# Cross-attention keys of the sample sequences loaded in 128-byte pieces and transposed by the vector engine, with three smaller edits

## The chip, the cores and the metric

The kernel runs on one core of a Trainium2 chip. A core has the engines PE (TensorE: matrix products), DVE (VectorE), ACT (ScalarE) and POOL (GpSimd), a sync engine SP, and 16 DMA engines. Each engine works through its own list of instructions in order. The metric is the device time of one execution in microseconds (us).

## The reference, cut to what matters

One step of a hybrid decoder layer, for a prompt of 256 tokens and for eight sample sequences of 4 tokens each (288 tokens in all, d_model 2048). An SSD branch and a GLA branch, both with a state per sample sequence, are merged by gates; then cross-attention into 256 memory tokens per sequence, then a ConvFFN (2 x 5632 columns, a convolution over 3 rows, the first two being carried rows from a state).

```python
def _cross_attend(hn, mem_k, mem_v, w_cq, w_co):
    q = (hn @ w_cq).reshape(Bsz, L, CROSS_HEADS, CROSS_HEAD_DIM)     # 4 heads of 512
    s = jnp.einsum('blhd,bmhd->bhlm', q, mem_k) * (CROSS_HEAD_DIM ** -0.5)
    pr = jax.nn.softmax(s, axis=-1)
    o = jnp.einsum('bhlm,bmhd->blhd', pr, mem_v)
    return o.reshape(Bsz, L, D_MODEL) @ w_co
# prompt: mem_k, mem_v computed from mem_prompt; samples: cache_mem_k, cache_mem_v (8, 256, 4, 512), read from memory
```

All data are float32. The keys are stored token by token, with the 512 numbers of a head side by side. The scores need the sum over these 512, and PE sums over partitions, so each key tile of 128 tokens x 128 numbers has to be transposed.

## The kernel before, in words

All large products are projections: `proj` loads a weight tile over SP's queue (512 KB, 24 matmuls of 128 x 288), splits it into a high and a low part (ACT L103, DVE L105) and multiplies each with the activations (L147, L148, L151). The stages follow each other: the input projection with the SSD scan, the GLA scan, the gates and the mix, the cross-attention, and the FFN. The work of the scans is woven into projections, which run in the background: a generator yields after a piece of work, and `weave` (L172) takes as many background units, of 12 matmuls each, as the numbers N_MAIN and N_BG (L38, L39) ask for. A scheduler then orders the instructions of each engine; the final order is fixed when the kernel is built.

Cross-attention is `attend(hd)` (L1379), once for each of the four heads, with the projections of the queries (w_cq) and of the output (w_co) around it:

- `loads` is the list of a head's tiles of memory: the keys of eight sequences (kc), keys and values of the prompt (kp, vp) and the values of sequences 4 to 7 (vc). Each is one DMA on POOL of 512 KB (L1376), 128 partitions x 2 token tiles x 512 numbers, and lies in one of five buffers `x4` that all of these share. `rows()` keeps four ahead. The values of sequences 0 to 3 (vq, L1411) have a buffer of their own and are loaded on POOL too.
- each key tile is transposed by PE (`transpose_half`, L1346, with L1352): eight transposes of 128 x 128 into two PSUM tiles, which one DVE copy and one ACT copy bring to kT (L1409).
- `scores(q)` (L1397) multiplies four sequences at a time: for each of four d-tiles and each sequence j one matmul (L1401), which writes the 32 rows of PSUM partition group j.
- the prompt's keys are transposed by PE and multiplied (L1430 to L1432), softmax of the samples runs, the weights are transposed (L1454), and L1463 multiplies them with vc and vq; that frees the buffers of vc for the next head.

The other lines that the change touches: the GLA scan of a head reads the states of eight sequences in two halves, four buffers `sin` (L1036), which L1138 multiplies, L1147 and L1148 update, an SP DMA writes back, and a POOL DMA fills again for the second half. `nudge(n)` (L119) puts two transposes of the identity, with n rows, into PE's order; `nudge(72)` stands at L1276 behind the first half of the gates and `nudge(P)` (L1548) before the FFN. The carried rows of the FFN are loaded at L1523 into `fin` (eight DMAs on POOL, 88 KB each, in pieces of 128 bytes), turned by DVE at L1535 into `fst`, all at once, and used by `ffn_conv` in `ffn_up`. FFN columns are worked in six blocks, of up to 8 tiles (BLK). In the SSD scan the states are already loaded as `sqr` in pieces of 128 bytes (L727) and turned by a DVE transpose (L878): it transposes each 32 x 32 square of a tile in its place, so that the DMA has to bring the squares to their places.

Of the kernel before, what the change touches and what calls it, by code (L numbers as in the profile page):

```python
# [8 lines left out]
F32 = mybir.dt.float32  # L9
# [7 lines left out]
P = 128  # L17
# [3 lines left out]
NB = 8  # L21
NL = 4
NS = NB * NL
# [18 lines left out]
@with_exitstack  # L42
def hybrid_step(ctx: ExitStack, tc: tile.TileContext, I: dict, O: list):
# [222 lines left out]
    with pool("p0") as p0:  # L266
# [95 lines left out]
        r = 0  # L362
# [217 lines left out]
    def b2(name):  # L580
        return pa.tile([P, 512], F32, tag="b2", bufs=10, name=name)
# [447 lines left out]
    def gla_scan(h, eb, qe, ke, kd, kde, vT, sr):  # L1029
# [104 lines left out]
        for q in range(2):  # L1134
            for k in (1, 0):
                for j in (3, 2, 1, 0):
                    b = 4 * q + j
                    MM(osa[NS * j:NS * j + NS, :], qdm[:, k, b, :], sins[b][:, k, :], start=False,  # L1138
                       stop=(q == 1 and k == 0))
            yield  # L1140
            for b in range(4 * q, 4 * q + 4):
                sin = sins[b]
                kb = pa.tile([P, 256], F32R, tag="kb", bufs=2, name="kb")
                V.tensor_scalar(kb, kst, bmask[:, b:b + 1], None, ALU.mult)
                for k in range(2):
                    a = mm_tile()
                    MM(a, kb[:, k * P:(k + 1) * P], vst, start=True, stop=True)  # L1147
                    V.scalar_tensor_tensor(sin[:, k, :], sin[:, k, :], eb[:, k, SEQ + 4 * b + 3:SEQ + 4 * b + 4], a,  # L1148
                                           ALU.mult, ALU.add)
                    yield 1.25  # L1150
                nc.sync.dma_start(out=o_sgla[b, h].rearrange("(k p) v -> p k v", p=P), in_=sin)
# [96 lines left out]
    def bigr2(name):  # L1248
        return pb.tile([P, KT, T], F32R, tag="bigr2", bufs=2, name=name)
# [124 lines left out]
    def mem_rows(src, name):  # L1374
        t = x4(name)
        G.dma_start(out=t, in_=src.rearrange("(m p) d -> p m d", p=P))  # L1376
        return t

    def attend(hd):  # L1379


        xq = xqm[hd % 2]
        loads = [(I["cache_mem_k"][b, :, hd, :], "kc") for b in range(NB)]
        loads += [(o_pmk[0, :, hd, :], "kp"), (o_pmv[0, :, hd, :], "vp")]
        loads += [(I["cache_mem_v"][b, :, hd, :], "vc") for b in range(4, NB)]
        got = []
        vq = big.tile([P, 4, 2, 512], F32, tag="bigf", bufs=1, name="vq")

        def rows():
            while loads and len(got) < 4:  # L1390
                got.append(mem_rows(*loads.pop(0)))
            return got.pop(0)

        ssc = la_tile()
# [2 lines left out]
        def scores(q):  # L1397
            for d in range(4):
                for j in (3, 2, 1, 0):
                    b = 4 * q + j  # L1400
                    MM(ssc[NS * j:NS * j + NS, 0:256], xq[:, d, b, :], kT[b][:, d, :], start=(q == 0 and d == 0),  # L1401
                       stop=(q == 1 and d == 3))

        for b in range(NB):
            kc = rows()
            kT.append(k4("kT"))
            for d2 in range(2):
                a = transpose_half(kc, d2)
                (S.copy if d2 else V.tensor_copy)(kT[b][:, 2 * d2:2 * d2 + 2, :], a)  # L1409
# [95 lines left out]
    fst = pf.tile([P, FT, 2, 16], F32, name="fst")  # L1505
    hf = halves(bigr, "hf")
    h = bigf("h")
    for j2 in range(KT // 2):
# [10 lines left out]
    fin = pf.tile([P, FT, 32], F32, name="fin")  # L1519
    crows = I["state_ffn_conv"].rearrange("b k c -> (b k) c").rearrange("r (i t g p) -> i g r t p", i=2, g=4, p=32)  # L1520
    for i in range(2):
        for g in range(4):
            G.dma_start(out=fin[32 * g + 16 * i:32 * g + 16 * i + 16], in_=crows[i, g])  # L1523

    def ffn_cols():
        for i0 in (0, 4):
            a = mm_tile()
            for i in range(i0, min(5, i0 + 4)):
                TR(a[:, (i - i0) * P:(i - i0 + 1) * P], frow[:, i, :], ident)
            if i0 == 0:  # L1530
                V.tensor_copy(fcol, a.rearrange("p (a t) -> p a t", t=P)[:, :, 0:88])
            else:
                V.tensor_copy(gfin, a[:, 0:KT])
        for t0 in range(0, FT, 11):
            V.transpose(fst[:, t0:t0 + 11].rearrange("p t i r -> p (t i r)"),  # L1535
                        fin[:, t0:t0 + 11].rearrange("p t c -> p (t c)"))

    run(*wo[:5])
    late.append(ffn_cols)
# [42 lines left out]
    blocks = [(0, FT % BLK)] + [(b0, BLK) for b0 in range(FT % BLK, FT, BLK)]  # L1582

    def ffn_up(b0, n):
        pr = bigr2("pr")
        c = cin[(b0 + BLK - 1) // BLK % 2]
        for q0 in range(b0, b0 + n, 4):
            for j2 in range(2):
                av = [pf.tile([P, T], F32, tag="av", bufs=4, name="av") for _ in range(2)]

                def consa(j, a, j2=j2, av=av):
                    t = 2 * j2 + j
                    ffn_conv(q0 + t, a, av[j], fst[:, q0 + t, 0, :], c[:, 0, q0 - b0 + t, 0:18])

                def consg(j, a, j2=j2, av=av):
                    t = 2 * j2 + j
                    gv = pf.tile([P, T], F32, tag="gv", bufs=3, name="gv")
                    ffn_conv(FT + q0 + t, a, gv, fst[:, q0 + t, 1, :], c[:, 1, q0 - b0 + t, 0:18])
# [126 lines left out]
```

## Time and profile before

| | |
|---|---|
| median of 3 runs | 2558.31 us (2558.08 to 2559.57) |
| the profiled execution | 2558.59 us, its span 2556.9 us |
| mean granted clock of PE | 0.997 |
| DMA | 521.95 MB, mean 204 GB/s |
| POOL's DMA queue (q0) | 96.37 MB, 12.2% of the 16 engines' span |
| SP's DMA queue (q1) | 422.34 MB, 53.8% |

One execution is recorded by the hardware profiler. A row of the groups names line, engine, operation, output and input, the count, then busy us and mean ns of one, then the idle time of the engine ahead of it and what ended most of it. Matrix products of float32 count twice in the profile where they are made in two passes (L1352, L1401, L1463). The page's view of 40 slices (64 us each) shows what the DMA engines do along the span; slices 23 to 26 hold the cross-attention:

```profile
DMA  7766587776868585777666778755555555555553
GB/s 263 219 223 200 169 243 213 225 210 201 231 190 295 173 258 160 244 234 231 187 208 210 251 261 303 213 178 171 168 173 168 172 167 174 169 170 172 169 172 128
```

### The profile page before, as it was taken

The page shows a single profiled execution, that of the slowest core. Times are in us where ns is not written, and L with a number is a line of the kernel's source. Part 1 is how long each engine was busy: PE and PEld are TensorE (multiplying, and loading weights), DVE is VectorE, ACT ScalarE, POOL GpSimd, SP SyncE. Part 2 cuts the span into 40 slices and gives each one's busy share as a digit, 9 for nine tenths or more (in the row PEclk, how much of TensorE's full clock was granted, in tenths as well). Part 3 has the DMA queues.
Part 4 walks back from the last instruction along what each step waited for, and adds up shares of the span by engine and source line. Part 5 has one row for each costly group of instructions (what it writes and reads, how often), then busy time and mean ns, then how long its engine had stood idle before and what let it go on. Part 6 is the DMA issues. An engine that isn't in the chain of part 4 may idle for free.

```text
span 2556.9 us, 50431 instructions
## 1 busy us (share of the span) xinstructions
PE 2536.4 (99%) x18968; PEld 2438.1 (95%) x18968; DVE 1731.3 (68%) x3670; ACT 1351.5 (53%) x2712; POOL 380.1 (15%) x701
## 2 busy tenths in 40 slices
PE   9999999999999999999999999999999999999998
PEld 8889999999999999989999989899999999999998
DVE  6656777796867566766566555567777677675765
ACT  7656547646454554544455544456545455454545
POOL 3002234242200000010000122201010101010010
PEclk9999999999999999999999999999999999999999
DMA  7766587776868585777666778755555555555553
GB/s 263 219 223 200 169 243 213 225 210 201 231 190 295 173 258 160 244 234 231 187 208 210 251 261 303 213 178 171 168 173 168 172 167 174 169 170 172 169 172 128
DMA packets 441125, 521.95 MB, mean 204 GB/s; under 512 B 26492, under 2 KB 389212, under 8 KB 440816
## 3 DMA queue, kind: packets, MB, share of 16 engines
q1 hardware_dynamic: 407728, 422.34, 53.8%
q0 software_dynamic: 33120, 96.37, 12.2%
q8 instruction: 149, 2.44, 0.4%
q14 instruction: 96, 0.79, 0.1%
q10 hardware_dynamic: 32, 0.01, 0.0%
HBM read 473.13 MB, written 45.48 MB: 203 GB/s over the span
## 4 chain that ended last, share of the span: by engine, by line
PE 96%; DMA 2%; DVE 1%; ACT 0%; POOL 0%; issue 0%; DVEq 0%; POOLq 0%; ACTq 0%
PE acc L148 27%; PE acc L147 26%; PE acc L151 26%; PE acc L315 2%; PE acc L316 2%; PE acc L319 2%; PE mm L1352 1%; PE la L1138 1%; PE la L1401 1%; PE la L1463 1%; PE mm L1111 1%; PE mm L1147 1%; DMA raw<-in_w_co_dram 0%; DMA sin<-in_state_gla_dram 0%; DMA out_dram<-sin 0%
## 5 line engine op out<-in xcount | busy, mean ns | idle before, releaser
L105 DVE TENSOR_TENSOR wlo<-raw,whi 128x512 fp32r<-128x512 f32 x1464 | 997.4, 687 | 662.0 <-ACT whi L103 634.7
L103 ACT CAST whi<-raw 128x512 fp32r<-128x512 f32 x1464 | 896.8, 618 | 1017.9 <-PE acc L148 792.7
L147 PE MATMUL acc<-xn,whi 128*128 128x288 f32 (+1 forms) x1936 | 550.0, 299 | 0.0
L148 PE MATMUL acc<-xn,whi 128*128 128x288 f32 (+1 forms) x1936 | 542.0, 296 | 0.0
L151 PE MATMUL acc<-xn,wlo 128*128 128x288 f32 (+1 forms) x1936 | 414.1, 295 | 0.0
L148 PE MATMUL acc<-hf,whi 128*128 128x288 f32 x1408 | 393.1, 295 | 0.0
L147 PE MATMUL acc<-hf,whi 128*128 128x288 f32 x1408 | 389.0, 292 | 0.0
L147 PEld LDWEIGHTS acc<-xn,whi 128*128 128x128 f32 (+1 forms) x1936 | 364.4, 188 | 9.7 <-issue 7.2
L148 PEld LDWEIGHTS acc<-xn,whi 128*128 128x128 f32 (+1 forms) x1936 | 364.6, 188 | 6.6 <-issue 4.8
L151 PEld LDWEIGHTS acc<-xn,wlo 128*128 128x128 f32 (+1 forms) x1936 | 310.4, 188 | 1.4 <-issue 1.1
L151 PE MATMUL acc<-hf,wlo 128*128 128x288 f32 x1408 | 294.4, 290 | 0.0
L148 PEld LDWEIGHTS acc<-hf,whi 128*128 128x128 f32 x1408 | 264.5, 188 | 0.1
L147 PEld LDWEIGHTS acc<-hf,whi 128*128 128x128 f32 x1408 | 264.0, 188 | 0.1
L151 PEld LDWEIGHTS acc<-hf,wlo 128*128 128x128 f32 x1408 | 226.2, 188 | 0.0
L148 PE MATMUL acc<-pr,whi 128*128 128x288 f32 x704 | 196.5, 295 | 0.0
L147 PE MATMUL acc<-pr,whi 128*128 128x288 f32 x704 | 195.0, 293 | 0.0
L151 PE MATMUL acc<-pr,wlo 128*128 128x288 f32 x704 | 147.4, 290 | 0.0
L147 PE MATMUL acc<-un,whi 128*128 128x288 f32 x512 | 146.1, 301 | 1.1 <-DVE ma L955 1.0
L148 PE MATMUL acc<-un,whi 128*128 128x288 f32 x512 | 143.3, 295 | 0.0
L1551 POOL COPY fsp<-fst 128x16 f32<-128x16 f32 x88 | 36.2, 414 | 686.6 <-DVE av L1563 444.0
L148 PEld LDWEIGHTS acc<-pr,whi 128*128 128x128 f32 x704 | 132.3, 188 | 0.0
L147 PEld LDWEIGHTS acc<-pr,whi 128*128 128x128 f32 x704 | 132.0, 188 | 0.0
(508 smaller groups left out, 4329.1 us busy)
## 6 DMA issues: line engine op xcount, KB each, us to landing
raw<-in_w_in_dram SPq DMA_DIRECT2D x240, 512.0 KB
raw<-in_w_up_dram SPq DMA_DIRECT2D x176, 512.0 KB
raw<-in_w_down_dram SPq DMA_DIRECT2D x88, 512.0 KB
raw<-in_w_cv_dram SPq DMA_DIRECT2D x32, 512.0 KB
raw<-in_w_ssd_out_dram SPq DMA_DIRECT2D x32, 512.0 KB
sin<-in_state_gla_dram POOLq DMA_DIRECT2D x32, 512.0 KB, 6.1
out_dram<-sin SPq DMA_DIRECT2D x32, 512.0 KB
raw<-in_w_gla_out_dram SPq DMA_DIRECT2D x32, 512.0 KB
```

Source lines behind the costliest of these rows:

```text
L103: S.copy(hi, raw)
L105: V.tensor_tensor(lo, raw, hi, ALU.subtract)
L147: MM(a, hi[:, k, cs], xh, start=(k0 + s0 + k == 0), stop=False)
L148: MM(a, hi[:, k, cs], xl, start=False, stop=False)
L151: MM(a, lo[:, k, cs], xh, start=False, stop=(k0 + s0 + k == nk - 1))
L315: MM(accs[m], mn_hi[:, kk, ms_], hi[:, 0, :], start=(kk == 0), stop=False)
L316: MM(accs[m], mn_lo[:, kk, ms_], hi[:, 0, :], start=False, stop=False)
L319: MM(accs[m], mn_hi[:, kk, ms_], lo[:, 0, :], start=False, stop=(kk == KT - 1))
L1111: MM(a, kt[:, i, k * P:(k + 1) * P], vt[i], start=True, stop=True)
L1138: MM(osa[NS * j:NS * j + NS, :], qdm[:, k, b, :], sins[b][:, k, :], start=False, stop=(q == 1 and k == 0))
L1147: MM(a, kb[:, k * P:(k + 1) * P], vst, start=True, stop=True)
L1551: G.tensor_copy(sp[:, :, 0:2], st.rearrange("p (b k) -> p b k", k=2))
```

## The change

Four edits, in one diff. (Lines of the kernel after are a little further down: L1354 for L1352, L1419 for L1401, L1484 for L1463.)

1. Keys. For both halves q of the eight sequences (SQK = (1, 1)) a tile holds one d-tile (128 of the 512 numbers) of four sequences, not all 512 of one. `key_squares` loads it with four DMAs on POOL of 128 KB, each into 32 partitions, in pieces of 32 numbers (128 bytes), such that a DVE transpose of 32 x 32 squares completes the transposition. Two DVE transposes per tile write kT; the PE transposes of kc and their copies out of PSUM are gone. The scores of one d-tile need one tile now.
2. The last GLA head: `yield 3` behind the first half of its sample states, and N_BG of the last head 46 instead of 43.
3. `nudge(72)` is gone.
4. Carried rows: loaded and turned for each block of the FFN, two blocks ahead, in two buffers `fin` of 8 tiles.

```diff
+SQK = (1, 1)
-N_BG = [60] * 4 + [43] * 4
+N_BG = [60] * 4 + [43] * 3 + [46]
...
+            if h == 3 and q == 0:
+                yield 3
...
-    nudge(72)
...
-        loads = [(I["cache_mem_k"][b, :, hd, :], "kc") for b in range(NB)]
+        loads = []
+        for q in range(2):
+            if SQK[q]:
+                loads += [(q, d) for d in range(4)]
+            else:
+                loads += [(I["cache_mem_k"][b, :, hd, :], "kc") for b in range(4 * q, 4 * q + 4)]
...
+        def key_squares(q, d):
+            t = x4("kc")
+            r = I["cache_mem_k"][4 * q:4 * q + 4, :, hd, P * d:P * d + P].rearrange("b (y p) (g c) -> g p (b y) c", p=32, c=32)
+            for g in range(4):
+                G.dma_start(out=t[32 * g:32 * g + 32].rearrange("p a (y c) -> p (a y) c", c=32), in_=r[g])
+            return t
...
-                    b = 4 * q + j
-                    MM(ssc[NS * j:NS * j + NS, 0:256], xq[:, d, b, :], kT[b][:, d, :], start=(q == 0 and d == 0),
+                    k = kT[4 * q + d][:, j, :] if SQK[q] else kT[4 * q + j][:, d, :]
+                    MM(ssc[NS * j:NS * j + NS, 0:256], xq[:, d, 4 * q + j, :], k, start=(q == 0 and d == 0),
...
-                a = transpose_half(kc, d2)
-                (S.copy if d2 else V.tensor_copy)(kT[b][:, 2 * d2:2 * d2 + 2, :], a)
+                if SQK[b // 4]:
+                    V.transpose(kT[b][:, 2 * d2:2 * d2 + 2, :].rearrange("p b m -> p (b m)"), kc[:, d2, :])
+                else:
+                    a = transpose_half(kc, d2)
+                    (S.copy if d2 else V.tensor_copy)(kT[b][:, 2 * d2:2 * d2 + 2, :], a)
...
+    def carried_load(n):
+        if n < len(blocks):
+            b0, c = blocks[n]
+            fins.append(pf.tile([P, BLK, 32], F32, tag="fin", bufs=2, name="fin"))
+            for i in range(2):
+                for g in range(4):
+                    G.dma_start(out=fins[n][32 * g + 16 * i:32 * g + 16 * i + 16, 0:c], in_=crows[i, g, :, b0:b0 + c])
...
 def ffn_up(b0, n):
+        carried_load(nb + 2)
+        carried_turn(nb + 1)
```

The order on POOL, from the last loads of head 0 to those of head 1, before (kc are keys, vq and vc values of the samples, kp and vp keys and values of the prompt):

```order
L1376 DMA vc<-in_cache_mem_v_dram 128x2x512 x4
L1376 DMA kc<-in_cache_mem_k_dram 128x2x512 x5
L1411 DMA vq<-in_cache_mem_v_dram 128x2x512 x4
L1376 DMA kc<-in_cache_mem_k_dram 128x2x512 x3
L1376 DMA kp<-out_dram 128x2x512
L1376 DMA vp<-out_dram 128x2x512
L1376 DMA vc<-in_cache_mem_v_dram 128x2x512 x4
```

The same stretch after:

```order
L1378 DMA vc<-in_cache_mem_v_dram 128x2x512 x4
L1401 DMA kc<-in_cache_mem_k_dram 32x32x32 x19
L1432 DMA vq<-in_cache_mem_v_dram 128x2x512
L1401 DMA kc<-in_cache_mem_k_dram 32x32x32
L1432 DMA vq<-in_cache_mem_v_dram 128x2x512
L1401 DMA kc<-in_cache_mem_k_dram 32x32x32 x4
L1432 DMA vq<-in_cache_mem_v_dram 128x2x512
L1401 DMA kc<-in_cache_mem_k_dram 32x32x32 x4
L1432 DMA vq<-in_cache_mem_v_dram 128x2x512
L1401 DMA kc<-in_cache_mem_k_dram 32x32x32 x4
L1378 DMA kp<-out_dram 128x2x512
L1378 DMA vp<-out_dram 128x2x512
```

Eight key DMAs of a head have become 32, and the loads of vq stand between them.

PE's order in head 2, around the last sample keys, before (L147, L148 and L151 are projections, L1352 transposes, L1401 scores):

```order
L151 MATMUL acc<-hn_16181,wlo 128x288
L1352 MATMUL mm<-ident,kc 128x128 x4
L151 MATMUL acc<-hn_16181,wlo 128x288
L147 MATMUL acc<-hn_16181,whi 128x288
L1352 MATMUL mm<-ident,kp 128x128 x4
L148 MATMUL acc<-hn_16181,whi 128x288
L1352 MATMUL mm<-ident,kp 128x128 x4
L1401 MATMUL la<-kT,xqm_17406 32x256 x8
L147 MATMUL acc<-hn_16181,whi 128x288
L148 MATMUL acc<-hn_16181,whi 128x288
```

And PE's order in head 3 after, at the place of its last keys (L152 is a projection, L1419 scores, L1354 a transpose, L1451 to L1453 the prompt's scores):

```order
L152 MATMUL acc<-co_17399,wlo 128x288
L1419 MATMUL la<-kT,xqm_17404 32x256 x4
L152 MATMUL acc<-co_17399,wlo 128x288
L1419 MATMUL la<-kT,xqm_17404 32x256 x24
L1354 MATMUL mm<-ident,kp 128x128 x8
L1451 MATMUL mm<-kTh,qh 128x256
L1452 MATMUL mm<-kTl,qh 128x256
```

The transposes of kc are gone, the scores come in groups of four, one for each tile of keys, and the last 24 stand without projections between them. Between one L1484 (L1463 before) and the next, the order of before has 192, 192 and 169 projection matmuls, that of after 257, 114 and 48.

More of the change, by code (lines that the diff above doesn't have):

```diff
@@ L1390, in rows @@
             while loads and len(got) < 4:
-                got.append(mem_rows(*loads.pop(0)))
+                x = loads.pop(0)
+                got.append(key_squares(*x) if x[0] in (0, 1) else mem_rows(*x))
             return got.pop(0)
@@ L1504, in hybrid_step @@
     gfin = pf.tile([P, KT], F32, name="gfin")
-    fst = pf.tile([P, FT, 2, 16], F32, name="fst")
     hf = halves(bigr, "hf")
@@ L1517, in hybrid_step, with carried_turn @@
         G.dma_start(out=frow[0:88 if i < 4 else KT, i, :], in_=src.rearrange("(t p) -> t p", p=P))
-    fin = pf.tile([P, FT, 32], F32, name="fin")
+    blocks = [(0, FT % BLK)] + [(b0, BLK) for b0 in range(FT % BLK, FT, BLK)]
     crows = I["state_ffn_conv"].rearrange("b k c -> (b k) c").rearrange("r (i t g p) -> i g r t p", i=2, g=4, p=32)
-    for i in range(2):
-        for g in range(4):
-            G.dma_start(out=fin[32 * g + 16 * i:32 * g + 16 * i + 16], in_=crows[i, g])
+    fins, fsts = [], []
+    def carried_load(n):
[5 more added lines that the diff above has]
+                    G.dma_start(out=fins[n][32 * g + 16 * i:32 * g + 16 * i + 16, 0:c], in_=crows[i, g, :, b0:b0 + c])
+    def carried_turn(n):
+        if n < len(blocks):
+            c = blocks[n][1]
+            fsts.append(pf.tile([P, BLK, 2, 16], F32, tag="fst", bufs=3, name="fst"))
+            V.transpose(fsts[n][:, 0:c].rearrange("p t i r -> p (t i r)"), fins[n][:, 0:c].rearrange("p t c -> p (t c)"))
+    carried_load(0)
+    carried_load(1)
     def ffn_cols():
@@ L1533, in ffn_cols @@
                 V.tensor_copy(gfin, a[:, 0:KT])
-        for t0 in range(0, FT, 11):
-            V.transpose(fst[:, t0:t0 + 11].rearrange("p t i r -> p (t i r)"),
-                        fin[:, t0:t0 + 11].rearrange("p t c -> p (t c)"))
+        carried_turn(0)
     run(*wo[:5])
@@ L1580, in ffn_caches @@
                                 in_=st[32 * g + r0:32 * g + r1, i, 0:n])
-    blocks = [(0, FT % BLK)] + [(b0, BLK) for b0 in range(FT % BLK, FT, BLK)]
     def ffn_up(b0, n):
         pr = bigr2("pr")
+        nb = (b0 + BLK - 1) // BLK
+        fst = fsts[nb]
+        carried_load(nb + 2)
+        carried_turn(nb + 1)
         c = cin[(b0 + BLK - 1) // BLK % 2]
@@ L1592, in consa @@
                     t = 2 * j2 + j
-                    ffn_conv(q0 + t, a, av[j], fst[:, q0 + t, 0, :], c[:, 0, q0 - b0 + t, 0:18])
+                    ffn_conv(q0 + t, a, av[j], fst[:, q0 - b0 + t, 0, :], c[:, 0, q0 - b0 + t, 0:18])
                 def consg(j, a, j2=j2, av=av):
@@ L1597, in consg @@
                     gv = pf.tile([P, T], F32, tag="gv", bufs=3, name="gv")
-                    ffn_conv(FT + q0 + t, a, gv, fst[:, q0 + t, 1, :], c[:, 1, q0 - b0 + t, 0:18])
+                    ffn_conv(FT + q0 + t, a, gv, fst[:, q0 - b0 + t, 1, :], c[:, 1, q0 - b0 + t, 0:18])
                     S.activation(gv, gv, ACT.Silu)
```

## The prediction

> **What bounds the kernel now.** I read the page first, then the waits of PE.
>
> ```profile
> PE 2536.4 (99%) x18968; PEld 2438.1 (95%) x18968; DVE 1731.3 (68%) x3670; ACT 1351.5 (53%) x2712; POOL 380.1 (15%) x701
> PE 96%; DMA 2%; DVE 1%; ACT 0%; POOL 0%; issue 0%; DVEq 0%; POOLq 0%; ACTq 0%
> ```
> ```profile
> PE mm L890 <- ACT cst L603: 3.5, 1, 3.5
> PE la L1138 <- DMA sin<-in_state_gla_dram: 2.0, 1, 2.0
> PE mm L1648 <- DVE h L1635: 1.2, 1, 1.2
> ```
> PE is busy for 99% of the span, carries 96% of the chain, and its longest wait is 3.5 us. So work taken from PE shortens the kernel, unless PE then has to wait. The place is the memory attention, four heads between 1430 and 1630 us. Its chain, with start and length in us:
>
> ```profile
> 1481.13 3.57 PE la L1463 x32
> ...
> 1505.73 1.86 PE la L1401 x32
> 1507.93 0.87 PE mm L1352 x8
> ...
> 1518.54 1.00 PE la L1401 x16
> 1529.79 3.57 PE la L1463 x32
> ```
> L1463 multiplies a head's weights with its values, L1401 makes the scores, L1352 transposes keys. From L1463 to L1463 a head takes 1529.79 - 1481.13 = 48.7 us, and PE never waits in it. Eight transposes take 0.87 us, 0.109 us each. In the stretches of one head the transfers are heavy in the first and lighter in the second half (the columns are the busy times of PE, PEld, DVE, ACT and POOL, the clock, the DMA share and GB/s):
>
> ```profile
> 1481.00:1505.00 24.00, 24.00 (x197) 21.30 (x196) 12.82 (x25) 10.29 (x21) 8.48 (x12) 1.00 0.97 338
> 1505.00:1530.00 25.00, 25.00 (x233) 22.12 (x235) 14.52 (x35) 11.79 (x25) 4.26 (x6) 1.00 0.72 226
> ```
> The second limit is therefore close: 24 us at 338 GB/s with the DMA engines 97% busy.
>
> **The change part by part.** The groups that bear on it (busy us and mean ns of one, then idle time before it and what ended that):
>
> ```profile
> L1352 PE MATMUL mm<-ident,kc 128*128 128x128 f32 x256 | 36.5, 272 | 0.0
> L1409 DVE COPY kT<-mm 128x512 f32<-128x512 f32 x32 | 22.0, 687 | 11.7 <-PE mm L1352 11.5
> L1409 ACT COPY kT<-mm 128x512 f32<-128x512 f32 x32 | 18.7, 585 | 30.4 <-PE mm L1352 30.4
> L878 DVE STREAM_TRANSPOSE st<-sqr 128x512 f32<-128x512 f32 x32 | 21.9, 697 | 0.0
> L1376 POOL DMA_DIRECT2D kc<-in_cache_mem_k_dram x32 | 22.7, 711 | 97.9 <-PE mm L1352 43.8 <-DVE pms L1448 24.1 <-PE la L1463 17.2
> L727 POOL DMA_DIRECT2D sqr<-in_state_ssd_dram x128 | 82.7, 653 | 51.6 <-ACT ea L797 26.6 <-DVE st L878 13.8 <-DMA sin<-in_state_ssd_dram 6.8
> ```
> **Transposes.** PE loses 256 x 0.109 = 27.9 us (64 per head, 7.0 us). The 32 + 32 copies out of PSUM become 64 DVE transposes of the form of L878: per head DVE pays 16 x 0.70 - 8 x 0.69 = 5.7 us more on 27.3 busy of 49, ACT 4.7 less. Both stay under PE; at nothing.
>
> **Key loads on POOL.** A tile of keys was one DMA of 0.71 us; it becomes four of 128 KB in pieces of 128 bytes, the kind of sqr (64 KB, 0.65 us). Per head POOL issues 32 x 0.65 + 10 x 0.71 = 27.9 us of DMAs, against 18 x 0.71 = 12.8. POOL works in order, and the row of kc names what it waits for: 17.2 us for L1463, which frees the value buffers that keys share. So of a head's 32 key DMAs, 4 can go ahead and 28 follow L1463 of the head before, with 4 loads of vq between: 28 x 0.65 + 4 x 0.71 = 21.0 us. Landing, in the last column:
>
> ```profile
> kc<-in_cache_mem_k_dram POOLq DMA_DIRECT2D x32, 512.0 KB, 6.0
> sqr<-in_state_ssd_dram POOLq DMA_DIRECT2D x128, 64.0 KB, 5.3
> fin<-in_state_ffn_conv_dram POOLq DMA_DIRECT2D x8, 88.0 KB, 9.7
> ```
> No row has pieces of this size and stride; I take kc's 6.0 (bounds: 5.3 for sqr, 9.7 for fin, both in pieces of 128 bytes). Behind the last landing come two transposes (1.4), the last tile's four score matmuls (0.5), and what lies between scores and the values, 1529.79 - 1519.54 = 10.3 us with projections as filler. With 0.5 until the first buffer is free, a head cannot take less than 21.0 + 6.0 + 1.4 + 0.5 + 10.3 + 0.5 = 39.7 us. Low end: a softmax without filler, estimated at 7 from those 10.3, gives 36. High end: landing 9.7 and some 1.6 us of POOL's waits give 45.
>
> **What PE has to fill that.** In the order a head of before holds 192 projection matmuls (169 in the last). The rows that set their time:
>
> ```profile
> 1221.00:1429.00 208.00, 208.00 (x1582) 208.00 (x1582) 125.99 (x227) 106.02 (x197) 16.79 (x27) 1.00 0.66 206
> 1733.00:2500.00 767.00, 767.00 (x5903) 767.00 (x5902) 549.12 (x1285) 395.47 (x844) 87.41 (x180) 1.00 0.55 171
> ```
> 208/1582 = 0.1315 and 767/5903 = 0.1299 us each; at 0.130 they are 25.0 us. The rest of a head is then 48.7 - 7.0 - 25.0 = 16.7 us. In the order of after 257, 114 and 48 projection matmuls stand between one L1484 (the old L1463) and the next: much of that work is now placed before and in head 0. PE's work is 33.4 + 16.7 = 50.1, 14.8 + 16.7 = 31.5 and 6.2 + 16.7 = 22.9 us. Against 39.7 it waits 0, 8.2 and 16.8, together 25.0 us (at 36: 17.6; at 45: 35.6). Into heads 0 and 1 I put 2 (0 to 4), since each score group stands at a fixed place in PE's order and its tile may be late there.
>
> **Clock.** A wait of PE is followed by a lower clock (the third last column):
>
> ```profile
> 1148.00:1152.00 4.00, 2.00 (x18) 0.42 (x16) 0.73 (x2) 0.61 (x1) 0.00 (x0) 0.91 1.05 384
> 1152.00:1156.00 4.00, 4.00 (x25) 3.11 (x18) 0.90 (x3) 1.21 (x2) 0.00 (x0) 0.67 0.48 169
> ```
> After 2.0 idle us the next 4 ran at 0.67, which costs 4 x 0.33 = 1.3. Two or three such waits per head in heads 2 and 3 are 5 x 0.8 = 4 us (0, if they are too short, to 8). The Trainium skill (TensorE: Matmul & The Clock Gate, Part 1) says that half rate comes after at least one idle window of about 3.4 us. By that, waits tile by tile of 2.6 us would cost no clock and the sum would be 4 us lower. The rows above speak against it: 2.0 us were enough for 0.67.
>
> **Last GLA head.** The wait and its chain:
>
> ```profile
> 1128.90 1.90 PE la L1138 x16
> ...
> 1142.00 8.19 DMA sin<-in_state_gla_dram
> 1150.23 2.69 PE la L1138 x16
> ```
> `yield 3` puts three units of 12 projection matmuls, 36 x 0.130 = 4.7 us, ahead of the second L1138. That covers the wait of 2.0, the 2.69 - 1.90 = 0.8, and part of the low clock: -3.0 (-2 to -3.8).
>
> **nudge(72)** puts two transposes behind the gate, just ahead of the 208 us of the first of the two rows, which ran at 0.1315 a matmul. If they run at 0.130 without it: -2.5; if not, 0 to +0.5. I take -1.
>
> **Carried rows.** Behind the last head, where 704 KB of fin were loaded at once:
>
> ```profile
> 1630.00:1660.00 30.00, 29.45 (x221) 28.70 (x220) 17.57 (x37) 13.57 (x29) 12.58 (x25) 1.00 0.92 211
> ```
> 221 matmuls at 0.130 are 28.7 of these 30 us, so at most 1.2 can be won there. Now each block of the FFN loads its rows with eight small DMAs, on a POOL busy 87 of 767 us, and turns them on a DVE busy 549. -0.4 (-1.2 to +0.5).
>
> **Sum**, on the profiled execution's 2558.6: -27.9 + 25.0 + 2 + 4 - 3.0 - 1 - 0.4 = -1.3. The median is 0.3 below that execution, so **2557 us**. Low ends (17.6, 0, 0, -3.8, -2.5, -1.2) give -17.8, so 2540; high ends (35.6, 4, 8, -2, 0.5, 0.5) give +18.7, so 2577.
>
> **The rivals.** *A: keys arrive in time.* The 25 us fall away if POOL's stretch is not what a head waits for, for instance if the filler reaches. For it: in before no head has a wait, and its keys share the buffers in the same way. Against: 48 matmuls for head 3 fill 6 us of a 21 us stretch. Then -27.9 - 3.0 - 1 - 0.4 = -32: 2526. Half of it, waits of 12 us: 2540.
>
> **B: slower, POOL waits for its own landings.** POOL's DMAs take eight semaphores in turn, so the ninth waits for the first; L727's row has 6.8 us of it. At a landing of 9.7 that is 1.2 us per DMA: 28 and 4 DMAs take 38.8 instead of 21.0, and a head (12.7 being its fixed parts above) 38.8 + 9.7 + 12.7 = 61 at worst. It decides once landing passes 8 x 0.65 = 5.2 us; at 8 us (1.0 each) a head is 32 + 8 + 12.7 = 52.7, waits are 2.6 + 21.2 + 29.8 = 53.6, the sum with 6 for the clock -27.9 + 53.6 + 6 - 3.0 - 1 - 0.4 = +27: 2586. For it are the engine times (packets, MB, share of 16 engines), in 440 to 460 with 16 sqr and 4 larger loads, then in 1481 to 1505:
>
> ```profile
> q0 software_dynamic: 906, 2.22, 37.5%
> ...
> sqr<-in_state_ssd_dram POOLq DMA_DIRECT2D x16, 64.0 KB, 5.6
> ```
> ```profile
> q0 software_dynamic: 1542, 5.64, 67.2%
> ```
> 2.22 MB in 7.5 us are 296 GB/s; 5.64 MB in 16.1 are 350. Half of the former being larger loads at 350, the 128-byte pieces ran at some 250, so a head's 4.19 MB of keys take 17 us of all engines, its other 5.24 MB 15, and 114 matmuls' weights (0.52 MB for 24) 7: 39 us, just at the 39.7. Any dearer piece passes that. The Trainium skill (DMA: Bandwidth & Descriptors, Latency and other measured facts) measures 207 GB/s at a row pitch of 512 KiB between partitions, less at larger ones. Keys lie at 8 KB between partitions and 256 KB within one, and no run here shows such a stride; at 207 the estimate would be 20 us for the keys, and the sum 5 us higher.
>
> **C: the rate of the FFN.** 0.1315 in place of 0.1299 over the 767 us is +9.4 on the forecast: 2567. nudge(P) at 1733 is kept, but what precedes it moves.
>
> **D: the change does half.** If scores and values are ready earlier than the 10.3 shows and half of the waits go: 2545.
>
> **How the numbers follow.** No change means within 0.2%, 5.1 us (2553.2 to 2563.4), about what a measurement can tell. Forecast 0.50, of which 0.17 faster, 0.19 same, 0.14 slower; A 0.15 and D 0.08, faster (0.01 same); B 0.15, slower; C 0.12, of which 0.04 same. That is 0.39 faster, 0.24 same, 0.37 slower. The range 2538 to 2586 leaves out most of A and half of B.
>
> **What would show it.** Right: no L1352 on kc; waits of PE la on DVE kT of some 25 us, in heads 2 and 3; there a clock below 1; POOL busy without gaps for some 21 us behind each L1484; L1138's wait gone. Wrong: PE waits under 10 us there (A), key landings over 8 us with POOL waiting for DMAs (B), or more than 0.131 us a matmul after 1733 (C).

## The result and the profile after

The changed kernel takes 2604.12 us (median of 5 runs) against 2558.31 us: a ratio of 1.0179, 95% interval 1.0166 to 1.0192, or some 46 us more. The prediction was 2557, with a range of 2538 to 2586; the time lies 18 us above that range. One of the five executions, the profiled one, ran in a slower state (2787.66 us, mean granted clock 0.842; the median of the other four is 2603.31), so the rows below are from a repeat of the same kernel (`again`, 2599.39 us).

The busy times of its page, and its longest waits of PE:

```profile
PE 2530.4 (97%) x18710; PEld 2418.8 (93%) x18710; DVE 1750.3 (67%) x3704; ACT 1334.8 (51%) x2680; POOL 477.9 (18%) x837
```
```profile
PE la L1419 <- DVE kT L1427: 42.6, 13, 6.4
PE mm L891 <- ACT cst L604: 3.1, 1, 3.1
```
PE now waits 42.6 us, in 13 pieces, for turned keys. The starts of the products with the values, one for each head:

```profile
1494.09 3.57 PE la L1484 x32
...
1557.20 1.98 PE la L1484 x16
...
1610.91 1.98 PE la L1484 x16
...
1664.69 4.60 PE la L1484 x32
```
Heads take 63.1, 53.7 and 53.8 us, where they took 48.7. The last product starts 40.5 us after 1624.23, its place before, and the span is 2597.7 - 2556.9 = 40.8 us longer. The stretch from the first product of the query projection to the first of the FFN, before and after (columns as in the prediction):

```profile
1417.30:1715.00 297.70, 296.95 (x2464) 274.67 (x2464) 171.98 (x354) 140.74 (x277) 65.44 (x100) 1.00 0.78 246
1411.60:1755.80 344.20, 293.96 (x2209) 257.12 (x2208) 190.69 (x385) 123.97 (x245) 159.15 (x228) 0.90 0.79 212
```
It begins 5.7 us earlier in this execution and is 46.5 us longer: the whole loss lies in the attention. PE's busy time there falls by only 3.0 us, although 27.9 us of transposes are gone, because the rest of its work ran at a mean clock of 0.90. PE is idle for 50.2 us where it was idle for 0.8, and 50.2 - 0.8 - 3.0 are the 46.5. The stretches up to the values of head 0, and of heads 1, 2 and 3:

```profile
1400.00:1494.00 94.00, 90.23 (x687) 84.67 (x685) 59.15 (x120) 42.13 (x78) 35.65 (x47) 0.98 0.84 223
1494.00:1557.00 63.00, 54.92 (x424) 47.10 (x423) 34.10 (x73) 19.86 (x42) 32.13 (x42) 0.92 0.83 227
1557.00:1611.00 54.00, 37.91 (x286) 28.41 (x288) 27.48 (x59) 13.79 (x30) 31.32 (x41) 0.78 0.88 227
1611.00:1665.00 54.00, 32.04 (x218) 21.55 (x214) 21.64 (x44) 9.16 (x21) 29.83 (x40) 0.70 0.85 213
```
PE is idle for 3.8, 8.1, 16.1 and 22.0 us, at a falling clock. Heads 2 and 3 move 227 and 213 GB/s at a DMA share of 0.88 and 0.85; the halves of a head before moved 338 at 0.97 and 226 at 0.72. So each byte takes more of the engines' time. The groups of the keys (busy, mean ns, idle before), and their landing:

```profile
L1401 POOL DMA_DIRECT2D kc<-in_cache_mem_k_dram x128 | 100.1, 788 | 57.5 <-DVE sm L1345 14.1 <-DVE wlo L106 9.0 <-PE la L1484 7.3
L1427 DVE STREAM_TRANSPOSE kT<-kc 128x512 f32<-128x512 f32 x64 | 41.4, 688 | 41.0 <-DMA kc<-in_cache_mem_k_dram 40.8 <-issue 0.2
```
```profile
kc<-in_cache_mem_k_dram POOLq DMA_DIRECT2D x128, 128.0 KB, 6.9
```
DVE turns a half tile in 0.69 us, as forecast, and what it waits for is mostly the DMA. In head 3 the chain runs thus:

```profile
1610.91 1.98 PE la L1484 x16
1613.04 8.01 DMA kc<-in_cache_mem_k_dram
...
1625.50 6.51 DMA vq<-in_cache_mem_v_dram
...
1633.78 9.11 DMA kc<-in_cache_mem_k_dram
1643.18 7.29 DMA kc<-in_cache_mem_k_dram
1650.59 1.32 DVE kT L1427 x2
1651.95 1.12 PE la L1419 x8
```
From the values to the last scores 41.0 us pass. That the chain names landings doesn't mean that POOL stood still: the first of the 28 key and 4 value DMAs behind the products starts at 1613.04, the last is issued by 1643.96, and of these 30.9 us POOL is busy with issuing for some 25. The other 6 are mostly waits for its own landings:

```profile
POOL kc L1401 <- DMA kc<-in_cache_mem_k_dram: 2.7, 3, 1.4
POOL kc L1401 <- DMA vq<-in_cache_mem_v_dram: 2.6, 3, 1.3
```
In the trace POOL's DMAs signal on eight semaphores in turn, and each of these waits ends 0.3 to 0.6 us after the eighth DMA before has landed. Two stretches show what the DMA engines do, the load stretch of head 3 and the end of head 2:

```profile
1611.00:1651.00 40.00, 21.89 (x168) 13.78 (x160) 15.01 (x26) 5.35 (x11) 28.41 (x38) 0.73 1.02 246
1605.00:1609.00 4.00, 4.00 (x32) 3.91 (x31) 3.92 (x15) 3.33 (x9) 0.31 (x1) 0.96 0.00 0
```
While keys load, the DMA engines are full (1.02) and PE is busy for 21.9 of 40 us; at the head's end the DMA engines stand still (0.00). The next four key DMAs start at 1608.69, and the other 28 from 1613.04 on, when the products with the values free their buffers.

### The profile page after: what moved, and what is told of

It reads as the page before. It is cut to its first block, busy times and chain, and to the rows that moved or that the text cites. A ratio compares the mean times of both kernels' runs of the same rounds, so it can differ in the third digit from the quotient of the medians.

```text
span 2786.0 us, 50106 instructions
## 1 busy us (share of the span) xinstructions
PE 2723.6 (98%) x18710; PEld 2590.9 (93%) x18710; DVE 1759.6 (63%) x3704; ACT 1338.0 (48%) x2680; POOL 478.6 (17%) x837
## 3 DMA queue, kind: packets, MB, share of 16 engines
q1 hardware_dynamic: 407728, 422.34, 49.9%
## 4 chain that ended last, share of the span: by engine, by line
PE 94%; DMA 3%; POOL 1%; DVE 1%; issue 0%; ACT 0%; DVEq 0%; ACTq 0%; POOLq 0%
PE acc L148 27%; PE acc L149 26%; PE acc L152 26%; PE acc L316 2%; PE acc L317 2%; PE acc L320 2%; DMA raw<-in_w_cq_dram 1%; DMA vq<-in_cache_mem_v_dram 1%; DMA kc<-in_cache_mem_k_dram 1%; POOL kc L1401 1%; PE la L1139 1%; PE mm L1148 1%; PE mm L1112 1%; PE la L1484 0%; PE la L1419 0%
## 5 line engine op out<-in xcount | busy, mean ns | idle before, releaser
L148 PE MATMUL acc<-xn,whi 128*128 128x288 f32 (+1 forms) x1936 | 582.3, 314 | 0.0
L149 PE MATMUL acc<-xn,whi 128*128 128x288 f32 (+1 forms) x1936 | 573.8, 308 | 0.0
L152 PE MATMUL acc<-xn,wlo 128*128 128x288 f32 (+1 forms) x1936 | 435.9, 308 | 0.0
L149 PE MATMUL acc<-hf,whi 128*128 128x288 f32 x1408 | 421.5, 311 | 0.0
L148 PE MATMUL acc<-hf,whi 128*128 128x288 f32 x1408 | 411.1, 305 | 0.0
L148 PEld LDWEIGHTS acc<-xn,whi 128*128 128x128 f32 (+1 forms) x1936 | 373.4, 193 | 11.7 <-issue 10.1
L149 PEld LDWEIGHTS acc<-xn,whi 128*128 128x128 f32 (+1 forms) x1936 | 369.7, 191 | 8.5 <-issue 6.0
L152 PEld LDWEIGHTS acc<-xn,wlo 128*128 128x128 f32 (+1 forms) x1936 | 322.5, 192 | 1.7 <-issue 1.3
L152 PE MATMUL acc<-hf,wlo 128*128 128x288 f32 x1408 | 319.1, 307 | 0.0
L148 PEld LDWEIGHTS acc<-hf,whi 128*128 128x128 f32 x1408 | 273.6, 194 | 0.1
L152 PEld LDWEIGHTS acc<-hf,wlo 128*128 128x128 f32 x1408 | 236.4, 196 | 0.0
L149 PE MATMUL acc<-pr,whi 128*128 128x288 f32 x704 | 210.3, 310 | 0.0
L148 PE MATMUL acc<-pr,whi 128*128 128x288 f32 x704 | 206.4, 306 | 0.0
L152 PE MATMUL acc<-pr,wlo 128*128 128x288 f32 x704 | 159.3, 307 | 0.0
L148 PE MATMUL acc<-un,whi 128*128 128x288 f32 x512 | 154.0, 314 | 0.0
L149 PE MATMUL acc<-un,whi 128*128 128x288 f32 x512 | 151.0, 307 | 0.0
L148 PEld LDWEIGHTS acc<-pr,whi 128*128 128x128 f32 x704 | 136.6, 194 | 0.0
```

Source lines behind the costliest of these rows:

```text
L148: MM(a, hi[:, k, cs], xh, start=(k0 + s0 + k == 0), stop=False)
L149: MM(a, hi[:, k, cs], xl, start=False, stop=False)
L152: MM(a, lo[:, k, cs], xh, start=False, stop=(k0 + s0 + k == nk - 1))
```

## The experiments

Each run is compared with runs of the kernel before on the same chip, some 2557 us; the ratio stands behind the time. "Keys' engine time" below is worked out from one row for each kernel, the traffic of POOL's queue between 1400 and 1660 us (packets, MB, share of 16 engines). For `no_key_edit`, where keys load as before:

```profile
q0 software_dynamic: 11520, 39.12, 45.1%
```
45.1% of 260 us are 117.3 us for 39.12 MB, so 334 GB/s, and the four heads' 16.78 MB of keys take 50.2 us, 12.6 per head. For the change:

```profile
q0 software_dynamic: 11488, 36.25, 54.8%
```
These are 142.5 us; the 19.47 MB that aren't keys take 58.3 at 334 GB/s, which leaves 84.2 for the keys: 21.0 per head, 199 GB/s. These are estimates: they hold the rest at 334 GB/s in every kernel.

**again** is the change without an edit.

> The changed kernel once more, for a profile at full clock. Theory P (POOL: 32 key DMAs of 0.79 us per head, with waits for landings between them) expects a head of 53 to 55 us from one L1484 to the next in heads 2 and 3, waits of PE for DVE kT of 60 to 75 us in the attention, granted clock 0.5 to 0.8 in the stretches with waits, and about 2602 us. Theory E (the 16 DMA engines are slow on 128-byte pieces) expects the same total with a DMA share near 1.00 at under 250 GB/s through the whole of a head. Theory O (projections moved ahead of head 0 are missing as filler later) expects next to no wait until head 1 and nearly all of it in heads 2 and 3.

It took 2599.39 us. Heads 2 and 3 came out at 53.7 and 53.8, as P has them; the share of the engines is full only while keys load, and not through the whole of a head, as E has it; and 12 of the 50 us of idle time lie in heads 0 and 1, which doesn't fit O well. The waits for turned keys (42.6) and all idle time from 1400 to 1665 (49.9) stayed under P's 60 to 75.

**no_key_edit**

```diff
-SQK = (1, 1)
+SQK = (0, 0)
```

> SQK = (0, 0): the keys as before; the yield in the last GLA head, the missing nudge(72) and the carried rows as in the change. All theories put the loss on the keys and expect 2552 to 2557 (the prediction's -3.0 - 1 - 0.4 = -4.4); over 2563 one of the three small edits costs by itself.

2556.74 us, 0.9995 (0.9985 to 1.0005): the keys are the whole loss. The three other edits together are not told from nothing. The second product of the last GLA head does lose its wait:

```profile
1127.25 1.85 PE la L1139 x16
1149.96 1.85 PE la L1139 x16
```
1.85 us now, 2.69 and a wait of 2.0 before. The rate behind the gate did not answer to nudge(72). From `no_key_edit`, the stretch behind the gate and the FFN:

```profile
1215.00:1375.00 160.00, 160.00 (x1218) 160.00 (x1217) 96.31 (x173) 81.00 (x150) 8.27 (x14) 1.00 0.67 203
1730.00:2490.00 760.00, 760.00 (x5849) 760.00 (x5848) 545.61 (x1278) 390.89 (x834) 90.74 (x188) 1.00 0.56 171
```
0.1314 and 0.1299 us a matmul, both as before.

**The form of the loads.** Six kernels change only `key_squares`. All six bring PE other numbers than the keys that the scores need, so they tell of time alone. In the change it reads:

```python
r = I["cache_mem_k"][4*q:4*q+4, :, hd, P*d:P*d+P].rearrange("b (y p) (g c) -> g p (b y) c", p=32, c=32)
for g in range(4):
    G.dma_start(out=t[32*g:32*g+32].rearrange("p a (y c) -> p (a y) c", c=32), in_=r[g])
```

*big_pieces*:

```diff
+r = I["cache_mem_k"][4*q+d, :, hd, :].rearrange("(m g p) c -> g p m c", m=2, p=32)
+    G.dma_start(out=t[32*g:32*g+32], in_=r[g])
```

> As the changed kernel, four key DMAs of 128 KB per tile into 32 partitions each, but in pieces of 2 KB, so the keys that PE sees are other numbers (wrong scores). Same count of DMAs, same bytes. Theory P expects little change, 2590 to 2605, since POOL still issues 32 per head and waits for landings. Theory E expects most of the loss gone: 2535 to 2560.

2586.68 us, 1.0117 (1.0096 to 1.0137). Between the two expectations: the pieces of 128 bytes are a part of the loss, not most of it.

*one_dma*:

```diff
+r = I["cache_mem_k"][4*q:4*q+4].rearrange("b (y p) h (k c) -> k (p h) (b y) c", p=32, c=32)
+G.dma_start(out=t.rearrange("p a (y c) -> p (a y) c", c=32), in_=r[4*hd+d])
```

> As the changed kernel, one key DMA of 512 KB per tile into 128 partitions, in pieces of 128 bytes at the same stride of 256 KB within a partition; the pieces are other ones (wrong scores). Same bytes and pieces, a quarter of the DMAs. Theory P expects POOL to be free (8 issues per head) and 2535 to 2565. Theory E expects no change, 2590 to 2610.

2573.14 us, 1.0064 (1.0044 to 1.0084). Again between; one DMA of 4096 pieces keeps POOL for 1.69 us.

*old_loads*:

```diff
+G.dma_start(out=t, in_=I["cache_mem_k"][4*q+d, :, hd, :].rearrange("(m p) d -> p m d", p=P))
```

> The changed kernel with each tile of keys loaded as before (one DMA of 512 KB, pieces of 2 KB, one sequence), then turned by DVE as in the change, so the scores are of other numbers. PE still loses the 27.9 us of transposes. If the form of the loads is the whole loss: 2526 to 2536. If the closed buffers cost even with the old loads (27 us of loading and 14 behind them, against 42 us of PE work): 2536 to 2550. If DVE's turn itself is what PE waits for: over 2570.

2536.70 us, 0.9925 (0.9896 to 0.9954). That is at the border of the first two expectations. So the transposes are worth some 20 us when keys load as they did, and waits of PE for the turn by DVE come to 2.7 us. The form of the loads, together with the order of PE's work that the scheduler gives with it (195, 189 and 171 projections between the values of the heads), is the loss, 63 to 67 us of it.

*four_wide* (the source of one_dma, cut into four):

```diff
+for g in range(4):
+    G.dma_start(out=t.rearrange("p a (y c) -> p (a y) c", c=32)[:, 8*g:8*g+8, :], in_=r[4*hd+d][:, 8*g:8*g+8, :])
```

> Four key DMAs of 128 KB per tile as in the change, pieces of 128 bytes at 256 KB stride, but each into all 128 partitions (8 pieces in each) instead of 32 (32 pieces in each); other numbers. The change 2599 to 2604, one DMA per tile into 128 partitions 2573. If the narrow destination is what costs: 2570 to 2578. If the count of DMAs is: 2595 to 2605.

2575.00 us, 1.0059 (1.0032 to 1.0087). The narrow destination costs. The count, beside such pieces, costs next to nothing against one_dma, whose order of projections differs (285, 220, 48, here 259, 113, 48).

*four_kb*:

```diff
+r = I["cache_mem_k"][4*q+d, :, hd, :].rearrange("(m p) d -> p m d", p=P)
+    G.dma_start(out=t[:, g//2, 256*(g%2):256*(g%2)+256], in_=r[:, g//2, 256*(g%2):256*(g%2)+256])
```

> Four key DMAs of 128 KB per tile into all 128 partitions, pieces of 1 KB; other numbers. Only the count of the change is left. If the count costs little: 2528 to 2545. If POOL's 32 issues per head with eight in flight cost by themselves: 2575 to 2590, near the 2587 of the pieces of 2 KB into 32 partitions.

2555.98 us, 0.9997 (0.9983 to 1.001), between the two. With large pieces, the kernel with 32 key DMAs per head is 19 us slower than old_loads with 8, at about the same engine time:

```profile
q0 software_dynamic: 13115, 39.16, 44.4%
```
PE waits 12.7 us for turned keys here and 2.7 in old_loads. POOL's longer row of issues (theory P) would do that, but the order of the projections differs too (320, 149, 48), and no run separates the two.

*spread32*:

```diff
-    G.dma_start(out=t[32*g:32*g+32].rearrange("p a (y c) -> p (a y) c", c=32), in_=r[g])
+    G.dma_start(out=t[g::4].rearrange("p a (y c) -> p (a y) c", c=32), in_=r[g])
```

> The changed kernel, each key DMA into 32 partitions as there, but every fourth partition (g, g+4, ...) instead of 32 neighbours; what DVE turns is then another arrangement (wrong scores). If the cost of the narrow destination is that all engines write to 32 neighbouring partitions at once: 2570 to 2580, as with four DMAs into 128 partitions. If it is that a DMA has only 32 partitions, whichever they are: 2597 to 2606.

2574.93 us, 1.0068 (1.0036 to 1.01). This is the sharpest pair: PE's order has the same 257, 114 and 48 projections, count, bytes and pieces are the same, and only the partitions of a DMA are not neighbours. 24 to 29 us go (the intervals of the two ratios lie apart), and the engine time falls with them:

```profile
q0 software_dynamic: 12696, 38.94, 51.5%
```
POOL's issue takes 0.786 us as before, but the keys land sooner, and in head 3 POOL hardly waits for them:

```profile
kc<-in_cache_mem_k_dram POOLq DMA_DIRECT2D x128, 128.0 KB, 5.3
...
POOL kc L1401 <- DMA kc<-in_cache_mem_k_dram: 0.9, 1, 0.9
POOL kc L1401 <- DMA vq<-in_cache_mem_v_dram: 0.5, 1, 0.5
```
From the values to the last scores 33.8 us pass there, not 41.0. That fits one account of the full engines and POOL's waits: slower transfers land later, and later landings hold up the issues behind them.

All beside each other, engine time worked out as above:

| kernel | DMAs per tile | partitions of each | piece | keys' engine us per head | us |
|---|---|---|---|---|---|
| no_key_edit (PE transposes) | 1 | 128 | 2 KB | 12.6 | 2556.7 |
| old_loads | 1 | 128 | 2 KB | 11.5 | 2536.7 |
| four_kb | 4 | 128 | 1 KB | 12.1 | 2556.0 |
| one_dma | 1 | 128 | 128 B | 17.3 | 2573.1 |
| four_wide | 4 | 128 | 128 B | 16.9 | 2575.0 |
| spread32 | 4 | 32, every fourth | 128 B | 16.9 | 2574.9 |
| big_pieces | 4 | 32 neighbours | 2 KB | 18.3 | 2586.7 |
| the change | 4 | 32 neighbours | 128 B | 21.0 | 2599 to 2604 |

Neighbouring partitions add 4 to 6 us of engine time per head; small pieces add 5 to 6 over 128 partitions and 2.7 beside neighbouring ones. The effects on the time don't add either: four DMAs go with 19 us beside large pieces and 2 beside small ones. What remains from spread32 to old_loads, 38 us, is not divided among pieces, issues and order. The scheduler gave some of these kernels another order of projections (195, 189, 171 in old_loads, 320, 149, 48 in four_kb), so only spread32 and four_wide are compared with the change at an equal or nearly equal order.

**pinned**: what the order does.

```diff
-MM(a, hi[:, k, cs], xh, start=(k0 + s0 + k == 0), stop=False)
+mm = MM(a, hi[:, k, cs], xh, start=(k0 + s0 + k == 0), stop=False)
+if pin and j == 0 and k == 0:          # only in the attention
+    tc.keep_in_program_order(mm)
```

> The changed kernel with one projection matmul of each unit of 12 held in program order in the attention, so that 192, 192 and 153 projection matmuls stand between the values of one head and the next (257, 114 and 48 in the change); the same DMAs. Theory O (the order: filler spent too early) expects most of the loss gone, 2540 to 2565. Theory L (a head's loads: they run only from the reading of the values to the last key, some 40 us, and 14 us follow) expects three heads of 54 to 57 from an earlier start, 2578 to 2592.

2604.11 us, 1.0181 (1.0147 to 1.0216): no gain, so the order alone (theory O) is not the loss. The values' products in its chain:

```profile
1482.01 1.98 PE la L1487 x16
1544.23 3.57 PE la L1487 x32
1605.92 3.57 PE la L1487 x32
1661.94 3.57 PE la L1487 x32
```
Head 0 ends 12 us earlier, and heads 1 to 3 take 62.2, 61.7 and 56.0. Projections kept as filler bring their weights, and these share the full engines with the keys; that is the likely reason, and no run takes the weights away. L missed too, with its heads of 54 to 57 and 2578 to 2592.

**buffers7** and **pinned_buffers7**: more tiles under way.

```diff
-return px.tile([P, 2, 512], F32, tag="x4", bufs=5, name=name)
+return px.tile([P, 2, 512], F32, tag="x4", bufs=7, name=name)
-return px.tile([P, 4, 256], F32, tag="k4", bufs=5, name=name)
+return px.tile([P, 4, 256], F32, tag="k4", bufs=3, name=name)
-while loads and len(got) < 4:
+while loads and len(got) < 6:
```

> The changed kernel with seven buffers x4 instead of five and three k4 instead of five, and six tiles kept ahead instead of four; order of the projections as in the change. Theory L, with closed buffers as the reason that DMA idles in a head's last 14 us, expects two tiles of keys to load there, a quarter of the 22 us that the engines give to a head's keys: heads of 48 to 49, 2580 to 2588. Theory O expects 2595 to 2602.

2586.24 us, 1.0111 (1.0083 to 1.014), in L's range, though its heads of 48 to 49 did not come. The heads:

```profile
1498.19 3.57 PE la L1484 x32
...
1560.43 1.93 PE la L1484 x15
...
1604.85 1.93 PE la L1484 x15
...
1646.36 5.23 PE la L1484 x32
```
Heads 2 and 3 take 44.4 and 41.5 instead of 53.7 and 53.8; head 1 stays at 62.2. The closed buffers are part of the loss.

> Both: the held order and seven buffers. If the two add, 2560 to 2575. If the DMA engines are then the floor (22 us for keys, 15 for values and the prompt's tiles, 12 for 192 matmuls' weights, 49 us per head, as long as a head of before), not under 2555. Theory O alone expects the same as the held order by itself.

2591.80 us, 1.0133 (1.0109 to 1.0157): the two don't add, and O alone, which expects the time of the held order by itself (2604), fails again.

**half_keys**

```diff
-SQK = (1, 1)
+SQK = (0, 1)
```

> SQK = (0, 1): sequences 0 to 3 as before, 4 to 7 in pieces of 128 bytes. PE loses 14 us of transposes, the engines get 5 more per head (44 of 48.7 in all), and 16 key DMAs follow the values instead of 28. Theory L expects the load stretch to fit in what PE has until head 2, and waits of 5 to 10 in head 3 where 48 projections are left: 2545 to 2560. If loads in small pieces cost in proportion (half of the change's +43), 2575 to 2582.

2577.50 us, 1.0082 (1.0057 to 1.0108). Half of the keys, half of the loss: the second expectation held, that of L failed.

**sp_queue**

```diff
-G.dma_start(out=t[32*g:32*g+32].rearrange("p a (y c) -> p (a y) c", c=32), in_=r[g])
+nc.sync.dma_start(out=t[32*g:32*g+32].rearrange("p a (y c) -> p (a y) c", c=32), in_=r[g])
```

> The changed kernel, its key DMAs issued on SP's queue between the weights, values still on POOL. If POOL's issuing (0.79 us each) and its waits for earlier landings bind: 2545 to 2575. If the DMA engines bind through the narrow 128-byte pieces, or the weights now wait behind keys: 2595 to 2640.

2607.52 us, 1.0202 (1.0173 to 1.0232). Taking the issues from POOL is no help, but the run doesn't clear POOL: SP's own issuing of keys (L1401) makes 25.6% of the chain between 1400 and 1700 us.

**warm**: does the low clock cost time?

```diff
+if hd >= 2 and b < 7:
+    a = mm_tile()
+    for n in range(16):
+        TR(a[:, n % 4 * P:n % 4 * P + P], kT[b][:, n % 4, n // 8 * P:n // 8 * P + P], ident)
```

> The changed kernel with 16 idle PE transposes (1.75 us at full clock, of kT into a PSUM tile that nothing reads) behind each of the first seven key tiles of heads 2 and 3, in the time in which PE waits for the next tile. The path stays as it is. If the lower clock behind the waits costs time on the path (13.6 us from the last scores to the values in head 3 against 10.3 before): 4 to 9 us less than the change, 2591 to 2597. If waits absorb it: 2599 to 2604; above that the idle transposes delay tiles themselves.

2602.28 us, 1.0177 (1.0136 to 1.0218). Heads 2 and 3:

```profile
1557.00:1611.00 54.00, 48.05 (x379) 39.48 (x378) 25.11 (x50) 10.77 (x24) 31.11 (x41) 0.91 0.93 234
1611.00:1668.00 57.00, 46.15 (x360) 37.45 (x358) 25.68 (x56) 13.10 (x29) 32.10 (x42) 0.91 0.84 203
```
The clock was 0.91 instead of 0.78 and 0.70, PE was busy for 24 us more, and the time stayed. So PE has slack there, and with two executions (2598.48 and 2606.07) no cost of the low clock can be told from zero.

**two_queues** and **two_queues_buffers7**: two groups of partitions at a time.

```diff
-G.dma_start(out=t[32*g:32*g+32].rearrange("p a (y c) -> p (a y) c", c=32), in_=r[g])
+(nc.scalar if g % 2 else G).dma_start(out=t[32*g:32*g+32].rearrange("p a (y c) -> p (a y) c", c=32), in_=r[g])
```

> The changed kernel with the key DMAs of g = 1 and 3 issued by ACT instead of POOL, so that two groups of 32 partitions are written from two queues at a time, and POOL issues 16 key DMAs per head. If that eases both the neighbours (the change 2602, spread partitions 2575) and the count (one DMA 2537, four 2556, with large pieces): 2570 to 2588. If ACT's waits for buffers hold up its other work: over 2600.

> The same with seven buffers x4, which took 16 us off the change. If both add: 2555 to 2572, about the kernel before at best. Under 2552 it would beat both kernels.

2612.78 us, 1.022 (1.0172 to 1.0269), and 2610.90, 1.0213 (1.0157 to 1.0269). PE's waits for keys shrank to 5.0 us, and others took their place. From `two_queues`, ACT between 1400 and 1670, then PE between 1400 and 1690:

```profile
ACT os L1500 <- DMA vq<-in_cache_mem_v_dram: 18.1, 1, 18.1
...
ACT co L189 <- DMA kc<-in_cache_mem_k_dram: 13.3, 1, 13.3
```
```profile
PE mm L1494 <- DVE co L190: 28.3, 3, 13.3
PE la L1419 <- ACT os L1500: 13.6, 1, 13.6
```
ACT stood at key DMAs, and its copies came late. The order of the projections is another one too (286, 218, 48, and 176, 204, 196 with seven buffers). Whether two queues would ease the engines stays open. None of the versions that keep the reference's keys and turn them by DVE beats the kernel before.

## Why the prediction was wrong, point by point

- *Transposes, -27.9.* Right in kind: old_loads is 20 us faster. Its trace shows where the other 8 are, in the attention stretch that takes 297.70 us before:

```profile
1414.30:1690.70 276.40, 270.84 (x2210) 247.29 (x2209) 185.92 (x385) 123.54 (x245) 81.67 (x132) 1.00 0.79 264
```
  PE's busy time fell by 26.1 us, and PE waits 5.6 us where it waited 0.8. (The 256 rows of L1352 are 64 transposes for each of four heads, so these count once; the remark ahead of the prediction that they count twice holds for L1401 and L1463 only.)
- *"A head cannot take less than 39.7 us."* This is the step that failed, and in it the 21.0 us for POOL's stretch of issues. Up to the last scores its terms gave 0.5 + 21.0 + 6.0 + 1.4 = 28.9 us; in head 3 of `again` 41.0 pass. They are 2.1 until the first buffer is free, 30.9 until the last key DMA is issued, 6.5 until it has landed, and 1.5 for the turn. Of the 9.9 us that the stretch of issues is longer, 3.9 come from an issue of 0.788 us in place of 0.65, and 6.0 from POOL's waits between issues, 5.3 of them for its own landings, which the forecast put at nothing here (1.6 at its high end). From the last scores to the values 12.7 us pass where 10.8 were forecast, which makes the head 53.8. That keys issued behind the values meet a PE out of filler was right; the size was 14 us per head too small. In `four_kb`, with 32 issues as well, the last head takes 1618.28 - 1578.38 = 39.9 us, but that it equals the 39.7 is luck: with its own issue of 0.543 and landing of 4.9 the sum gives 35.6. From its chain:

```profile
1578.38 1.98 PE la L1484 x16
...
1618.28 4.86 PE la L1484 x32
```
- *The price of keys on the engines.* 17 us per head were taken from sqr at 250 GB/s; by the estimate above they were 21.0 at 199. The larger slip was to hold the engines' 39 us against a whole head of 39.7. Loads run mostly until the last key, at a DMA share of 1.02 in head 3, and then the engines come to stand still. So most of the 39 us belonged into the load stretch, with turn, scores and softmax behind them: up to 39 + 1.4 + 0.5 + 10.3 = 51, and the measured heads have 54. That sum could have been made from the rows that the prediction quoted.
- *What I left out.* The destination: each of the four DMAs writes 32 neighbouring partitions, and spread32 shows that to cost 24 to 29 us.
- *Rival B* came nearest: heads of 52.7 forecast, 53.7 and 53.8 measured; 2586 forecast, 2599 to 2604 measured. Its mechanism is in the trace: landings of 6.9 us (median) are longer than eight issues of 0.788, 6.3, and POOL waits for the eighth DMA before. Its terms were 32 us for the issues, 8 for the landing and 12.7 for the rest; head 3 shows 30.9, 6.5 and 16.3, so that its 52.7 is near in part by luck. It missed head 1, 63.1 in place of 52.7, whose chain goes by another way:

```profile
1513.54 18.32 DMA raw<-in_w_cq_dram
...
1533.22 1.31 DVE kT L1427 x2
1534.57 1.08 PE la L1419 x8
```
  A weight tile takes 18.3 us to land there, and the turn of the keys stands behind that tile's split in DVE's order. So the loads also cost time by making weights late, which neither the forecast nor a rival names.
- *Clock, +4.* A lower clock came (0.78 and 0.70 in heads 2 and 3). It stretched PE's work in the attention by some 25 us (294.0 against 297.0 - 27.9), six times the 4, but at no cost in time that `warm` could show: where PE is slower, it waits less. The wait from the last scores to the values in head 3, 13.6 us in the expectation of `warm`, is 11.6 in the trace of `again`. The Trainium skill (TensorE: Matmul & The Clock Gate, Part 1) wants an idle window of about 3.4 us for half rate; waits here reached 6.4 us, so these rows agree with it, and they don't decide on the 2.0 us of before.
- *GLA, nudge, carried rows, -4.4.* The GLA wait is gone as forecast; the sum of the three is -0.1 us between medians, -3.8 to +1.3 by the interval, so less than forecast, and not told from zero. In the one execution traced of each, the attention begins 5.7 us earlier in `again` and 3.8 in `no_key_edit` than before, but the medians show nothing of that. The FFN kept its 0.1299 (rival C did not come).

On the neighbours, the Trainium skill (SBUF — State Buffer, Door 1: The DMA port swizzle) states that DMA bandwidth goes by how many of 16 ports the partitions reach, and that partitions 0 to 31 reach eight of them. Every fourth partition reaches all 16 by its formula. Spread32 against the change agrees with that in direction (16.9 against 21.0 us of engine time); no run here shows the ports themselves.

## What to carry to other kernels

When a load changes its form, price it by engine time per byte at its own piece size and its own destination partitions, and set that against the stretch in which loads may run, between the release of their buffers and their use, not against the whole period. Where an engine's DMAs go round a fixed number of semaphores, compare the landing with that many issues. A layout that saves PE work by cutting DMAs into 32 neighbouring partitions and 128-byte pieces can cost the DMA engines more than it saves PE, as here. Filler moved into a wait need not help when its own transfers share the resource that is waited for.

## What the runs showed of the hardware

- A DMA on POOL cost issue time by its pieces: 0.54 us for 128 KB in pieces of 2 KB or 1 KB, 0.79 for 1024 pieces of 128 bytes into 32 partitions (0.89 into 128), 1.69 for 4096.
- POOL's DMAs signal on eight semaphores in turn. In head 3 of `again`, with landings of some 7 us against eight issues of 6.3, POOL waited 5.3 us for them; in spread32, with landings of 5.3, it waited 1.4.
- 32 neighbouring partitions cost the DMA engines, by the estimate above, some 1.5 times as much for pieces of 2 KB as 128 partitions do (18.3 against 11.5 and 12.6 us per head), and 1.24 times for pieces of 128 bytes (21.0 against 16.9). Every fourth partition cost no more than all 128 (16.9).
- Pieces of 128 bytes cost 1.4 to 1.5 times as much as large ones over 128 partitions (16.9 and 17.3 against 11.5 and 12.1), about what sqr's rows had given.
- Idle transposes in PE's waits raised the clock of heads 2 and 3 from 0.78 and 0.70 to 0.91, and no change in the time could be told.
